# Shifting the SBUF pools of a decoder layer by pads: activations on multiples of 64 bytes, weight tiles 32 bytes off

## Chip, core and metric

The kernel is one layer of a decoder and runs on one core of a Trainium2 chip. The metric is the device time of the whole kernel in microseconds; lower is better. Everything is computed in float32; matmuls take operands of type float32r, and each product is made of three (high x high, high x low, low x high) to keep the precision, so every matrix is held as a high and a low part.

## What is computed

The reference, cut to what matters (one sequence of 1024 tokens, width 1024, 8 heads, depth 1):

```python
h = rms_norm(x, attn_norm_w)
q, k, v, u, g = jnp.split(h @ w_in, splits, axis=-1)
q, k = rms_norm(q, q_norm_w), rms_norm(k, k_norm_w)      # per head, two halves of 64
a = diff_attention(q[0], q[1], k[0], k[1], v, lam, rel_bias)   # softmax 1 - lam * softmax 2
a = rms_norm(a, subln_w) * (1.0 - lam_init)
y_a = a @ w_proj_attn
u_a, u_b = jnp.split(u, 2, axis=-1)
c = causal_depthwise_conv(u_a * sigmoid(u_b), conv_w, conv_b)   # width 31
y_b = silu(layer_norm(c, conv_ln_w, conv_ln_b)) @ w_proj_conv
g_a, g_b = jnp.split(sigmoid(g + gate_b), 2, axis=-1)
x = x + (g_a * y_a + g_b * y_b) @ w_out
gt, up = jnp.split(rms_norm(x, ffn_norm_w) @ w_gate_up, 2, axis=-1)
return x + (silu(gt) * up) @ w_down
```

## The kernel before

A matmul here multiplies a moving tile (streamed, 128, 256 or 512 columns) with a stationary tile of 128 x 128 (the weights of TensorE, loaded by a LDWEIGHTS that may run beside the matmul before it). Two helpers issue nearly all of them through `mm3` (lines 144 to 146, three matmuls: high x high, high x low, low x high of the two operands, each step of k):

- `gemm_T(w, mhi, mlo, sb)`: the matrix from DRAM (whi, wlo) is stationary, the activations move, 512 columns. It serves the U items (convolution input, 8 items, each 2 x 2 x 24 matmuls), the G items (gates, 16 items of 2 x 24), the two projections (aT and cT, 384 each), and the first three gate and up blocks of the FFN (288).
- `gemm_N(o, halves, shi, slo, i)`: the activations are stationary and whi, wlo move, 256 columns. It serves the V items (4 of 192), the Q items (8 of 192) and the output projection (mT, 768).

The FFN's other 19 blocks run in `pair` (products in line 1153), which makes four blocks of the gate and up products out of seven products of 12 matmuls each: three with parts of h2 moving (h2 is the normalised second input, tiles h_hi and h_lo), three with the differences T1 to T3 moving against weights split into whi and wlo, and one with T4 moving against weights in the tiles sh and sl. The down projection (1056 matmuls) has the hidden activations in whi and wlo as weights, and sh and sl, 512 columns of w_down, moving.

The stages in order: V and U items with the first Q item (to about 330 us); attention (330 to 840), in which the scores of head h run while Q and G items of later heads fill TensorE's gaps; the projection of the attention (840 to 940); that of the convolution (940 to 1030); the output projection (1030 to 1130); the second norm (to 1145) and the FFN (1145 to 1575); the down projection (to the end).

In attention a step (h, i) issues: `scores`, two score matmuls per 512 keys (sc, weights qs, moving ks, lines 684 and 685), a reduction on VectorE (E, mn), an exponential on ScalarE (E, l, line 691) and their difference on VectorE; `turn`, transposes of E (pT) and their split into ph (ScalarE, line 111) and pl (VectorE, line 116); every second step `weigh` (pW, moving ph and pl, weights vh and vl), and two steps later `back`, a transposition (pB) whose result ScalarE scales into an (line 748) and squares with a row sum (line 749). A Q item projects q and k of a head: after each bank pg of 512 columns ScalarE copies it to qkraw (line 563) and squares it in eight parts of 64 columns, with row sums (line 566); the bank is free again when the last of the eight is done. In attention two banks go round for pg. The squares themselves are never read, only their sums are: they go to scratch tiles, jk in `q_item` and jk2 in `back`, one buffer each, in the pool sm.

The program is recorded in the order of the code, and a scheduler then orders the instructions of each engine, within the dependencies of the tiles. Two instructions that write the same buffer of sm keep the order in which they were recorded.

Where tiles lie: SBUF pools are laid one behind the other in the order in which they are opened, from the left (cst, big, wp, sm, and then the pool of the stage: a0, attn, b1, fp), or one ahead of the other from the right end (the convolution's, then q and k; later aT and mT; later the differences T). In the program as built, hT_hi begins at byte 18368 of each partition, hT_lo at 51136 (cT and h2 take the same places later), wraw at 83904, whi at 92096, wlo at 104384, sg at 116672; the first tile of the stage's pool on the left is at 123552, and aT, mT and T begin at 163808. Divided by 64, hT, cT, h2, wraw, whi, wlo and sg leave 0; all tiles of the stage pools on the left (E, ph, vh, sh, sl and others) and all on the right (aT, mT, T, qs, ks) leave 32. Every operand of a matmul lies a multiple of 512 bytes behind the start of its tile, so the remainder of the tile is that of the operand.

Of the kernel before, what the change touches and what calls it, by code (L numbers as in the profile page):

```python
# [9 lines left out]
F32 = mybir.dt.float32  # L10
F32R = mybir.dt.float32r
AF = mybir.ActivationFunctionType
# [3 lines left out]
P = 128  # L16
# [3 lines left out]
HD = 64  # L20
VD = 128
# [33 lines left out]
def kernel(  # L55
# [36 lines left out]

    cst = ctx.enter_context(tc.tile_pool(name="cst", bufs=1))
    big = ctx.enter_context(tc.tile_pool(name="big", bufs=1, reuse_waits="tile"))
    wp = ctx.enter_context(tc.tile_pool(name="wp", bufs=3, reuse_waits="tile"))
    sm = ctx.enter_context(tc.tile_pool(name="sm", bufs=4))
    dr = ctx.enter_context(tc.tile_pool(name="dr", bufs=1, space=bass.MemoryType.DRAM))
    ps = ctx.enter_context(tc.tile_pool(name="ps", bufs=2, space=PSUM))

    bg = Spread()  # L100
    uid = [0]

    def nm(s):
        uid[0] += 1
        return f"{s}_{uid[0]}"

    def f32(ap):
        return ap.bitcast(F32)
# [21 lines left out]
    def pg():  # L130
        npg[0] += 1
        p_, tag = pgs[npg[0] % len(pgs)]
        return p_.tile([P, 512], F32, tag=tag, name=nm("pg"))
# [4 lines left out]
    def pm(z="pm"):  # L138
        npm[0] += 1
        p_, tag = pms[npm[0] % len(pms)]  # L140
        return p_.tile([P, 512], F32, tag=tag, name=nm(z))
# [53 lines left out]
    def pcol(key, k=0):  # L195
        c = col[key] + k
        return pvec[:, c : c + 1]
# [104 lines left out]
    def gemm_T(w, mhi, mlo, sb):  # L302

        o = pg()
        cs = slice(sb * 512, (sb + 1) * 512)
        for k in range(NKT):
            mm3(o[:], w[0][:, k, :], w[1][:, k, :], kt(mhi, k)[:, cs], kt(mlo, k)[:, cs], k == 0, k == NKT - 1)
        return o

    def gemm_N(o, halves, shi, slo, i):  # L310

        ts = slice(i * P, (i + 1) * P)
        for k in range(NKT):
            whi, wlo = halves[k // 4]
            mm3(o, kt(shi, k)[:, ts], kt(slo, k)[:, ts], whi[:, k % 4, :], wlo[:, k % 4, :], k == 0, k == NKT - 1)
# [153 lines left out]
    def rstd_of(ss, n, scale, fast=False):  # L469
        v = sm.tile([P, 16], F32, tag="v", name=nm("v"))[:, :n]  # L470
        dve.tensor_scalar(v, ss, scale, EPS, op0=ALU.mult, op1=ALU.add)
        return rsq(v, n, fast)
# [79 lines left out]
    def q_item(h):  # L552
        halves = [ws.next(), ws.next()]
        t = {}
        T[h] = t
        for b in range(2):
            raw = qkp.tile([P, 4, 256], F32, tag="qkraw", name=nm("qkraw"), bufs=2)
            ss = sm.tile([P, 16], F32, tag="ss16", name=nm("ss16"))
            for i2 in range(2):
                o = pg()  # L560
                for e in range(2):
                    gemm_N(o[:, 256 * e : 256 * (e + 1)], halves, hT_hi, hT_lo, 4 * b + 2 * i2 + e)
                act.copy(raw[:, 2 * i2 : 2 * i2 + 2, :], o[:].rearrange("p (e c) -> p e c", c=256))
                jk = sm.tile([P, HD], F32, tag="jk", name=nm("jk"), bufs=1)
                for g in range(8):
                    act.activation(
                        jk[:], o[:, g * HD : (g + 1) * HD], AF.Square, accum_out=ss[:, 8 * i2 + g : 8 * i2 + g + 1]
                    )
                if i2 == 0:
                    yield  # L570
            r = rstd_of(ss[:], 16, 1.0 / HD, fast=h > 0)
            r4 = raw[:].rearrange("p i (g d) -> p (i g) d", d=HD)
            dve.tensor_tensor(r4, r4, r.unsqueeze(2).to_broadcast([P, 16, HD]), op=ALU.mult)

            def turn_qk(b=b, raw=raw):


                dma = nc.sync.dma_start
                for z, key in enumerate(("q", "k")):
                    pt = pm("pQ")  # L580
                    for i in range(4):
                        pe.transpose(pt[:, i * P : (i + 1) * P], raw[:, i, z * P : (z + 1) * P], ident[:])  # L582
                    w = pcol(key + "n")

                    def part(j):
                        return qkp.tile([P, 512], F32R, tag=f"{key}s{j}", name=f"{key}s{j}_{h}_{b}", bufs=2 if key == "q" else 3)

                    s1, s2 = part(1), part(2)
                    act.activation(s1[:], pt[:], AF.Identity, scale=w)
                    lo = part(3) if key == "q" else qkp.tile([P, 512], F32R, tag="klo", name=f"klo_{h}_{b}", bufs=1)  # L590
                    dve.scalar_tensor_tensor(lo[:], pt[:], w, f32(s1[:]), op0=ALU.mult, op1=ALU.subtract)
                    dma(f32(s2[HD:, :]), f32(s1[HD:, :]))
                    if key == "q":
                        lo2 = part(4)
                        for one, two in ((s1, s2), (lo, lo2)):
                            if one is lo:
                                dma(f32(two[HD:, :]), f32(one[HD:, :]))
                            dma(f32(two[:HD, :]), f32(one[HD:, :]))
                            dma(f32(one[HD:, :]), f32(one[:HD, :]))
                        t["q", b] = (s1, lo), (s2, lo2)  # L600
                    else:
                        dma(f32(s2[:HD, :]), f32(lo[HD:, :]))
                        dma(f32(s1[HD:, :]), f32(lo[:HD, :]))
                        t["k", b] = s1, s2

            late.append((NT * h if b and h else 0, turn_qk))
            yield

    inatt = [False]
    MAKE = {"V": v_item, "U": u_item, "Q": q_item, "G": g_item}  # L610

    def run(items):
# [124 lines left out]
    def back(h, b, ar):  # L737
        pt = pm("pB")
        for e in range(2):
            pe.transpose(pt[:, e * P : (e + 1) * P], ar[:, e * P : (e + 1) * P], ident[:])  # L740
        if h not in AN:
            AN[h] = aps.tile([P, NT, VD], F32, tag="an", name=f"an{h}", bufs=1)
            SSA[h] = sm.tile([P, NT], F32, tag="ssa", name=nm("ssa"))
        jk = sm.tile([P, VD], F32, tag="jk2", name=nm("jk2"), bufs=1)
        for e in range(2):
            i = 2 * b + e
            src, r = pt[:, e * P : (e + 1) * P], RL[h][:, i : i + 1]
            act.activation(AN[h][:, i, :], src, AF.Identity, scale=r)
            act.activation(jk[:], src, AF.Square, scale=r, accum_out=SSA[h][:, i : i + 1])
# [42 lines left out]
    def slot(n, nq):  # L792

        with after(last_fill[0]):
            for h, b, ar in ready(backs, n):
                back(h, b, ar)
                if b == NT // 2 - 1:
                    subln(h)
                    sublns.append((n + 1, h))
            for _ in range(nq):  # L800
                if late[0][0] <= n:
                    late.pop(0)[1]()
            for h in ready(sublns, n):
                subln_T(h)
            for h, b in ready(weighs, n):
                backs.append((n + 2, (h, b, weigh(h, b))))
                if b == NT // 2 - 1 and h + 1 < H:
                    load_v(h + 1)
# [153 lines left out]
    def gated(d, cs):  # L962
        g = bp.tile([P, 512], F32, tag="gt", name=nm("gt"), bufs=4)
        nc.sync.dma_start(g[:], d[:, cs])
        act.activation(g[:], g[:], AF.Sigmoid)
        return g
# [29 lines left out]
    for cl in ((0, 1, 2), (3, 4), (5, 6), (7,)):  # L996
        pair = [(c, ws.next()) for c in cl]
        for sb in range(2):
            cs = slice(sb * 512, (sb + 1) * 512)
            for c, w in pair:  # L1000
                g = gated(g_d[NKT + c], cs)
                ya = bp.tile([P, 512], F32, tag="ya", name=nm("ya"), bufs=4)
                nc.sync.dma_start(ya[:], ya_d[c][:, cs])
                o = gemm_T(w, cT_hi, cT_lo, sb)
# [32 lines left out]
    for z, (j, half) in enumerate(WO):  # L1037
# [3 lines left out]
        for i2 in (2 * half, 2 * half + 1):  # L1041
            o = pg()
# [22 lines left out]
    def acc():  # L1065
        nacc[0] += 1
        p_, tag = banks[nacc[0] % 4]
        return p_.tile([P, 512], F32, tag=tag, name=nm("acc"))
# [172 lines left out]
    for n in range(2):  # L1241
        o = [acc() for i in range(NT)]
# [62 lines left out]
```

## Time and profile before

| what | value |
|---|---|
| median of 3 runs | 1830.63 us (1829.6 to 1832.09) |
| profiled execution | 1831.76 us, span 1830.0 us |
| TensorE matmul busy | 1800.7 us (98%), 9895 records |
| TensorE weight load busy | 1556.9 us (85%) |
| VectorE, ScalarE, GpSimd busy | 1237.2, 752.8, 26.6 us |
| granted TensorE clock, mean | 0.993 |
| DMA queue of SyncE | 40.4% of 16 engines' span |

The span is the time from the first to the last profiled instruction of one execution; 1.8 us of its time lie outside. Matmuls are pipelined: each record lasts some 280 ns (256 columns) or 390 ns (512), but the next one begins before it ends. What a matmul costs in a dense stretch is therefore the distance from its start to the next start, which a window of a pure stage gives as its length divided by the number of matmuls in it. The mean duration of a group moves with the distance, since the part that overlaps stays nearly the same. "Idle before" is the time in which the engine had nothing to do ahead of a group's instructions, with what ended it.

### The profile page before, as it was taken

To read this page: it belongs to the slowest core of one execution; us is meant where nothing else is said; L and a number is where in the kernel's file an instruction comes from. 1 tells how busy PE (TensorE), PEld (TensorE's weight loads), DVE (VectorE), ACT (ScalarE), POOL (GpSimd) and SP (SyncE) were. 2 spreads that over 40 slices of the span, in tenths; PEclk is the share of its full clock that TensorE was granted. 3 is DMA by queue.
4 is the path that set the end of the run, shared out by engine and by line. 5 is a ranking of instruction groups with operands and counts; after the bars stand their busy time and mean duration, and the time that the engine had idled before them with its cause. 6 is when DMAs were issued, how large, how long until landed. Compare 5 with 4: busy or idle time off the path is not lost.

```text
span 1830.0 us, 26409 instructions
## 1 busy us (share of the span) xinstructions
PE 1800.7 (98%) x9895; PEld 1556.9 (85%) x9895; DVE 1237.2 (68%) x2157; ACT 752.8 (41%) x1814; POOL 26.6 (1%) x106
## 2 busy tenths in 40 slices
PE   7999999999999999999999999999999999899998
PEld 6899998999898989987888998788888888788887
DVE  6388789999888998884885337965565655433433
ACT  5211331667676876664473114322222222222221
POOL 3000000000000000000000000000000000000000
PEclk9999999999999999999999999999999999999999
DMA  8433273233544354436945424122232232544643
GB/s 243 153 116 121 93 208 103 81 103 110 139 127 126 93 135 125 119 106 236 304 135 157 157 93 139 58 84 77 75 96 72 75 98 69 184 138 138 230 140 113
DMA packets 218032, 236.56 MB, mean 129 GB/s; under 512 B 12160, under 2 KB 157608, under 8 KB 217904
## 3 DMA queue, kind: packets, MB, share of 16 engines
q1 hardware_dynamic: 215872, 228.64, 40.4%
q0 software_dynamic: 1744, 5.19, 1.0%
q8 instruction: 78, 1.28, 0.3%
q10 hardware_dynamic: 288, 1.05, 0.2%
q14 instruction: 50, 0.41, 0.1%
HBM read 158.24 MB, written 58.23 MB: 118 GB/s over the span
## 4 chain that ended last, share of the span: by engine, by line
PE 95%; DMA 2%; DVE 1%; ACT 1%; issue 0%; SPq 0%; ACTq 0%; DVEq 0%
PE acc L1153 20%; PE pg L144 17%; PE pg L146 17%; PE pg L145 17%; PE acc L144 5%; PE acc L145 4%; PE acc L146 4%; PE sc L685 2%; PE sc L684 2%; PE pT L720 2%; PE pW L144 1%; PE pW L146 1%; PE pW L145 1%; PE pQ L582 1%; DMA wraw<-in_w_in_dram 1%; PE pS L761 0%
## 5 line engine op out<-in xcount | busy, mean ns | idle before, releaser
L111 ACT CAST whi<-wraw 128x1024 fp32r<-128x1024 f32 x153 | 160.6, 1050 | 432.4 <-PE acc L145 159.3
L116 DVE TENSOR_TENSOR wlo<-wraw,whi 128x1024 fp32r<-128x1024 f32 x153 | 187.0, 1222 | 194.3 <-ACT whi L111 194.2
L393 DVE SCALAR_TENSOR_TENSOR acc<-u,cw,acc 128x1024 f32<-128x1024 f32 x240 | 306.9, 1279 | 2.8
L144 PE MATMUL pg<-whi,hT_hi 128*128 128x256 f32 x768 | 221.1, 288 | 0.1
L146 PE MATMUL pg<-whi,hT_lo 128*128 128x256 f32 x768 | 221.0, 288 | 0.1
L145 PE MATMUL pg<-wlo,hT_hi 128*128 128x256 f32 x768 | 220.2, 287 | 0.0
L144 PE MATMUL pg<-hT_hi,whi 128*128 128x512 f32 x512 | 201.3, 393 | 0.0
L145 PE MATMUL pg<-hT_lo,whi 128*128 128x512 f32 x512 | 201.1, 393 | 0.0
L146 PE MATMUL pg<-hT_hi,wlo 128*128 128x512 f32 x512 | 200.6, 392 | 0.0
L144 PEld LDWEIGHTS pg<-whi,hT_hi 128*128 128x128 f32 x768 | 148.2, 193 | 3.1 <-ACT gr L541 0.6
L146 PEld LDWEIGHTS pg<-whi,hT_lo 128*128 128x128 f32 x768 | 148.2, 193 | 2.7 <-DVE hT_lo L116 0.7
L145 PEld LDWEIGHTS pg<-wlo,hT_hi 128*128 128x128 f32 x768 | 148.2, 193 | 1.7 <-DVE wlo L116 0.3
L144 PE MATMUL acc<-sh,whi 128*128 128x512 f32 x352 | 138.7, 402 | 4.0 <-ACT sh L111 4.0
L145 PE MATMUL acc<-sl,whi 128*128 128x512 f32 x352 | 139.8, 397 | 0.0
L146 PE MATMUL acc<-sh,wlo 128*128 128x512 f32 x352 | 139.6, 397 | 0.0
L691 ACT ACTIVATE E<-E,mn 128x256 f32<-128x256 f32 (+7 forms) x128 | 99.9, 782 | 37.3 <-DVE mn L686 36.6
L146 PEld LDWEIGHTS pg<-hT_hi,wlo 128*128 128x128 f32 x512 | 96.2, 188 | 19.2
L144 PEld LDWEIGHTS pg<-hT_hi,whi 128*128 128x128 f32 x512 | 96.3, 188 | 18.9
L145 PEld LDWEIGHTS pg<-hT_lo,whi 128*128 128x128 f32 x512 | 96.3, 188 | 18.6
L111 ACT CAST whi<-s 128x1024 fp32r<-128x1024 f32 x38 | 39.9, 1049 | 142.3 <-PE acc L1153 108.3
L1153 PE MATMUL acc<-h_lo,whi 128*128 128x512 f32 x228 | 89.4, 392 | 0.0
L1153 PE MATMUL acc<-h_hi,whi 128*128 128x512 f32 x228 | 89.3, 392 | 0.0
(258 smaller groups left out, 4023.8 us busy)
## 6 DMA issues: line engine op xcount, KB each, us to landing
wraw<-in_w_gate_up_dram SPq DMA_DIRECT2D x44, 512.0 KB, 4.6
wraw<-gu_d SPq DMA_DIRECT2D x44, 512.0 KB, 3.7
wraw<-in_w_in_dram SPq DMA_DIRECT2D x40, 512.0 KB, 4.1
qs<-qs SPq DMA_DIRECT2D x96, 128.0 KB, 2.3
rd<-in_w_down_dram SPq DMA_DIRECT2D x44, 256.0 KB, 3.7
wraw<-in_w_in_dram SPq DMA_DIRECT2D x32, 256.0 KB, 3.5
g_d<-sgg SPq DMA_DIRECT2D x32, 256.0 KB, 2.2
gt<-g_d SPq DMA_DIRECT2D x32, 256.0 KB, 3.7
```

The source lines that it names most:

```text
L111: act.copy(dst, src)
L116: last_lo[0] = dve.tensor_tensor(dst, src, f32(hi), op=ALU.subtract).ins
L144: pe.matmul(o, lh, rh, start=start, stop=False)
L145: pe.matmul(o, lh, rl, start=False, stop=False)
L146: last_mm[0] = pe.matmul(o, ll, rh, start=False, stop=stop).ins
L393: dve.scalar_tensor_tensor(acc[0][:], us[c][:, t : t + S], cw[:, c, t : t + 1], acc[0][:], op0=ALU.mult, op1=ALU.add)
L582: pe.transpose(pt[:, i * P : (i + 1) * P], raw[:, i, z * P : (z + 1) * P], ident[:])
L684: pe.matmul(o[:, :w], qh[:, qs], k, start=True, stop=False)
L685: last_mm[0] = pe.matmul(o[:, :w], ql[:, qs], k, start=False, stop=True).ins
L691: act.activation(e[:, :nk], e[:, :nk], AF.Exp, bias=mn[:, j : j + 1], scale=-1.0, accum_out=l[:, j : j + 1])
L720: pe.transpose(pt[:, k * P : (k + 1) * P], e[:, (k0 + k) * P : (k0 + k + 1) * P], ident[:])
L1153: pe.matmul(o[:], a_[x_][:, k, :], b_[y_][:, k, :], start=start and k + x_ + y_ == 0, stop=k == 3 and x_ == 1, skip_group_check=not start,)
```

## The change

Three pads are added, and the two scratch tiles become one.

- A pool `shift` between big and wp holds one tile of 8 floats (32 bytes): wp and all behind it move by 32.
- cst gets 16 floats (64 bytes) more, at its start: big and all behind it move by 64.
- A pool `edge` of 24 floats (96 bytes) is the first on the right: all tiles on the right move down by 96.
- jk in `q_item` is now 128 columns wide, of which the first 64 are used, and jk in `back` has the same tag, so both share one buffer of 512 bytes where 256 and 512 bytes stood: what lies behind sm moves by -256.

```diff
     big = ctx.enter_context(tc.tile_pool(name="big", bufs=1, reuse_waits="tile"))
+    shift = ctx.enter_context(tc.tile_pool(name="shift", bufs=1))
+    shift.tile([P, 8], F32, name="pad_weights")
     wp = ctx.enter_context(tc.tile_pool(name="wp", bufs=3, reuse_waits="tile"))
...
+    cst.tile([P, 16], F32, name="pad_left")
+    edge = ctx.enter_context(tc.tile_pool(name="edge", bufs=1, side="right"))
+    edge.tile([P, 24], F32, name="pad_right")
...
-                jk = sm.tile([P, HD], F32, tag="jk", name=nm("jk"), bufs=1)
+                jk = sm.tile([P, VD], F32, tag="jk", name=nm("jk"), bufs=1)[:, :HD]
                 for g in range(8):
                     act.activation(
-                        jk[:], o[:, g * HD : (g + 1) * HD], AF.Square, accum_out=ss[:, 8 * i2 + g : 8 * i2 + g + 1]
+                        jk, o[:, g * HD : (g + 1) * HD], AF.Square, accum_out=ss[:, 8 * i2 + g : 8 * i2 + g + 1]
                     )
...
-        jk = sm.tile([P, VD], F32, tag="jk2", name=nm("jk2"), bufs=1)
+        jk = sm.tile([P, VD], F32, tag="jk", name=nm("jk"), bufs=1)
```

In the program as built, hT_hi then begins at 18432 and hT_lo at 51200, wraw at 84000, whi at 92192, wlo at 104480, sg at 116768, the stage's pool on the left at 123392, and aT, mT and T at 163712. Divided by 64, hT, cT and h2 leave 0 as before; wraw, whi, wlo and sg leave 32; the stage pools on the left and all tiles on the right leave 0. No instruction is added or removed. On TensorE, VectorE, ScalarE and SyncE the order differs from the one before in the attention stage, on TensorE first at the beginning of head 1, and in some places behind it up to the first products of the FFN; ahead of head 1 and behind those products nothing is moved but addresses. Lines behind the pads have numbers higher by 7.

## Prediction

> **What bounds the kernel now.** I read the page's busy shares and its chain first, then the stages by windows, then the matmul groups, then single matmuls.
>
> ```profile
> PE 1800.7 (98%) x9895; PEld 1556.9 (85%) x9895; DVE 1237.2 (68%) x2157; ACT 752.8 (41%) x1814; POOL 26.6 (1%) x106
> PE 95%; DMA 2%; DVE 1%; ACT 1%; issue 0%; SPq 0%; ACTq 0%; DVEq 0%
> ```
>
> TensorE is busy 98% of the span and carries 95% of the chain that ends last. All other engines together leave it idle for 1830.0 - 1800.7 = 29.3 us. So the time is the sum of the distances from one matmul to the next, and the change is worth what it does to those. Stages that are pure in one kind of matmul give the distance (the window, its length, PE busy with the count, then the other engines):
>
> ```profile
> 255.00:315.00 60.00, 60.00 (x266) 49.71 (x265) 51.79 (x46) 10.13 (x13) 0.60 (x4) 1.00 0.45 136
> 330.00:840.00 510.00, 506.64 (x3380) 463.92 (x3380) 444.33 (x1029) 343.92 (x1173) 11.69 (x65) 1.00 0.41 113
> 945.00:1025.00 80.00, 80.00 (x354) 66.28 (x353) 47.99 (x68) 35.06 (x53) 0.00 (x0) 1.00 0.44 138
> 1150.00:1195.00 45.00, 45.00 (x198) 37.19 (x197) 40.95 (x39) 13.98 (x17) 0.00 (x0) 0.99 0.19 59
> 1225.00:1560.00 335.00, 335.00 (x1453) 272.55 (x1452) 192.82 (x256) 92.47 (x120) 0.00 (x0) 1.00 0.27 82
> 1600.00:1820.00 220.00, 220.00 (x945) 177.35 (x944) 74.08 (x84) 59.80 (x76) 0.00 (x0) 1.00 0.44 150
> 162.00:183.00 21.00, 21.00 (x177) 21.00 (x176) 19.17 (x18) 2.04 (x5) 0.00 (x0) 1.00 0.35 113
> 1032.00:1098.00 66.00, 66.00 (x560) 66.00 (x559) 20.80 (x50) 9.80 (x12) 0.00 (x0) 1.00 0.41 144
> ```
>
> A record counts if any part of it lies in the window. A 512-column record lasts some 390 ns, so I take 1.7 off the count (390 / 227), and 2.4 for 256 columns (288 / 120). Then 512 columns take 60,000 / 264.3 = 227.0 ns with hT moving (255 to 315 us), 227.1 with cT, 229.2 with h2 in the gates, 230.8 in the FFN products, and 220,000 / 943.3 = 233.2 with sh and sl moving in the down projection. 256 columns take 120.3 ns with hT as weights and 118.4 with mT as weights. The clock is full in all of them and no window has PE idle but the attention's (3.4 us).
>
> Same shapes, different distances: what differs is where the two operands lie. I call a matmul **equal** if its moving tile and the weights loaded while it runs (those of the next matmul) start at the same remainder by 64 bytes, and **opposite** if the remainders differ by 32. In the kernel before, hT, cT, h2, whi and wlo are at 0; aT, mT, T, sh, sl, ph, vh, qs, ks and E at 32. The groups (busy us, mean ns of one):
>
> ```profile
> L145 PE MATMUL pg<-hT_lo,whi 128*128 128x512 f32 x512 | 201.1, 393 | 0.0
> L145 PE MATMUL pg<-cT_lo,whi 128*128 128x512 f32 x128 | 49.9, 390 | 0.0
> L145 PE MATMUL pg<-aTl,whi 128*128 128x512 f32 x128 | 50.8, 397 | 0.0
> L145 PE MATMUL acc<-sl,whi 128*128 128x512 f32 x352 | 139.8, 397 | 0.0
> L1153 PE MATMUL acc<-h_lo,whi 128*128 128x512 f32 x228 | 89.4, 392 | 0.0
> L1153 PE MATMUL acc<-T1l,whi 128*128 128x512 f32 x76 | 30.1, 396 | 0.0
> L145 PE MATMUL pg<-wlo,hT_hi 128*128 128x256 f32 x768 | 220.2, 287 | 0.0
> L145 PE MATMUL pg<-wlo,mTh 128*128 128x256 f32 x256 | 72.3, 282 | 0.0
> L145 PE MATMUL pW<-pl,vh 128*128 128x256 f32 x160 | 46.4, 290 | 0.0
> ```
>
> (Behind <- the moving tile comes first, the weights second.) With 512 columns, equal rows have 390 to 393 ns and opposite rows 396 to 397. With 256 it turns round: opposite (mT) 282, equal (hT, pW) 287 to 290.
>
> All these 512-column opposite rows have the moving tile at 32 and the weights at 0; the change makes the mirror image. The mirror image exists before only at seams. These are single matmuls, each asked for in a window of its own: two of cT, the last of cT, whose next weights are mT (32), and two of hT, the second followed by a score with weights qs (32).
>
> ```profile
> L144 PE MATMUL pg<-cT_hi,whi 128*128 128x512 f32 x1 | 0.4, 389 | 0.0
> L145 PE MATMUL pg<-cT_lo,whi 128*128 128x512 f32 x1 | 0.4, 389 | 0.0
> L146 PE MATMUL pg<-cT_hi,wlo 128*128 128x512 f32 x1 | 0.4, 397 | 0.0
> L146 PE MATMUL pg<-hT_hi,wlo 128*128 128x512 f32 x1 | 0.4, 389 | 0.0
> L145 PE MATMUL pg<-hT_lo,whi 128*128 128x512 f32 x1 | 0.4, 397 | 0.0
> ```
>
> The moving tile is the same; only the next weights have moved by 32, and the matmul is 8 ns longer. So I read the cost as one of opposite remainders, whichever side is shifted.
>
> **The change part by part.** The pads are allocated and never used: no instruction, no cost. They do what they say: hT, cT, h2 stay at 0 (18432 = 288 x 64), whi and wlo go to 32 (92192 = 1440 x 64 + 32), all pools behind them and on the right go to 0. So nearly every matmul becomes opposite.
>
> (a) 512 columns, equal to opposite, to 233.2 ns. U items, 768 matmuls x (233.2 - 227.0) = +4.8 us. Gate items, 768, in the attention stage, among scores and transposes: no window isolates them. Their group with U has 393 ns against 390 in pure stages, so the G half has some 396, against 397 for opposite rows: a lower bound of 1 ns, an upper one of 6.2; I take 4, +3.1, because the group's mean also holds matmuls that wait after transposes. cT, 384 x 6.1 = +2.3. Gates of the FFN, 288 x (233.2 - 229.2) = +1.2. Products: 19 pairs x 84 = 1596; of seven products three move h (equal now), three T against whi (opposite now), one T4 against sh. Afterwards six are opposite and T4 equal: (6 x 233.2 + 227) / 7 = 232.3 against 230.8, +2.4. Sum +13.8 (from 9 to 18, with every row at its lower or upper end).
>
> (b) 256 columns with hT as weights, equal to opposite: 118.4 - 120.3 = -1.9 ns. 960 outside attention, -1.8; 1344 inside, where I take half, -1.3. Sum -3.1 (from -4.4 to 0).
>
> (c) Opposite before, mirrored after: aT 384, sh 1056, mT 768: 0, give or take 2 ns each, 4 us. pW, scores and transposes: under 1 us.
>
> (d) ScalarE, VectorE and the queues also read shifted tiles. Before, both remainders exist:
>
> ```profile
> L111 ACT CAST whi<-wraw 128x1024 fp32r<-128x1024 f32 x153 | 160.6, 1050 | 432.4 <-PE acc L145 159.3
> L111 ACT CAST whi<-s 128x1024 fp32r<-128x1024 f32 x38 | 39.9, 1049 | 142.3 <-PE acc L1153 108.3
> rd<-in_w_down_dram SPq DMA_DIRECT2D x44, 256.0 KB, 3.7
> gt<-g_d SPq DMA_DIRECT2D x32, 256.0 KB, 3.7
> ```
>
> wraw and rd lie at 0, s and gt at 32, and the times agree: 0.
>
> (e) The scratch tile. The squares of q_item and of back write two tiles before and share one after. Nobody reads it, but its users must now run in the order of the program, and the scheduler moves the attention stage to fit. ScalarE near the end of head 0, before (qkraw is the copy of a projected bank pg, jk are its squares, E the exponentials of head 0):
>
> ```order
> L563 COPY qkraw_3835<-pg_3837 128x512
> L566 ACTIVATE jk_3887,ss_418_3836<-pg_3837 128x64 x3
> L691 ACTIVATE E_3623,l_3622<-E_3623,mn_3621 128x1024
> L566 ACTIVATE jk_3887,ss_418_3836<-pg_3837 128x64 x5
> L691 ACTIVATE E_3633,l_3622<-E_3633,mn_3621 128x1024
> ```
>
> The same place in the changed kernel, where that bank is called pg_3846 and its copy stands 17 rows ahead of its squares (an and jk from pB are back's scaling and squares, qs a part of the queries):
>
> ```order
> L755 ACTIVATE an_3430<-pB_3743,rl_0_2951 128x128
> L756 ACTIVATE jk_3746,ssa_3431<-pB_3743,rl_0_2951 128x128
> L755 ACTIVATE an_3430<-pB_3743,rl_0_2951 128x128
> L698 ACTIVATE E_3820,l_3813<-E_3820,mn_3812 128x256
> L756 ACTIVATE jk_3746,ssa_3431<-pB_3743,rl_0_2951 128x128
> L573 ACTIVATE jk_3896,ss_418_3845<-pg_3846 128x64
> L596 ACTIVATE qs_1_1_3756<-pQ_3751,pvec 128x512
> ```
>
> The eight squares that free the bank now stand behind back's. TensorE at the same place, before (pg the projection of the next Q item, sc the scores of head 1):
>
> ```order
> L146 MATMUL pg_3926<-whi_3547,hT_lo 128x256
> L144 MATMUL pg_4052<-whi_3379,hT_hi 128x256
> L145 MATMUL pg_4052<-wlo_3380,hT_hi 128x256
> L146 MATMUL pg_4052<-whi_3379,hT_lo 128x256
> L684 MATMUL sc_3812<-ks_1_0_3230,qs_1_0_3213 128x256
> L685 MATMUL sc_3812<-ks_1_0_3230,qs_1_0_3218 128x256
> ```
>
> TensorE there in the changed kernel (pT are transposes of E):
>
> ```order
> L153 MATMUL pg_3935<-whi_3556,hT_lo 128x256
> L691 MATMUL sc_3821<-ks_1_0_3239,qs_1_0_3222 128x256
> L692 MATMUL sc_3821<-ks_1_0_3239,qs_1_0_3227 128x256
> L727 MATMUL pT_3729<-ident,E_3632 128x128 x4
> L691 MATMUL sc_3919<-ks_1_0_3238,qs_1_0_3221 128x384
> ```
>
> The next bank's projection comes only 42 rows further on. Until then TensorE has ten score matmuls, transposes and the 24 of pW, some 7 us by the distances above. ScalarE has in that stretch, by the groups of the attention stage, a copy qkraw, three ph, four E (each with a read of the accumulator, 0.2 us), two each of an and of back's squares, qs, ks and ar, 7 to 9 us, and eight squares at 0.35 us (the starts of two), 2.8 us:
>
> ```profile
> L563 ACT COPY qkraw<-pg 128x512 f32<-128x512 f32 x27 | 15.8, 586 | 13.1 <-PE pg L146 13.1
> L111 ACT CAST ph<-pT 128x512 fp32r<-128x512 f32 x48 | 28.1, 586 | 27.3 <-PE pT L720 26.6
> L691 ACT ACTIVATE E<-E,mn 128x384 f32<-128x384 f32 x16 | 9.9, 618 | 0.8 <-DVE mn L686 0.7
> L749 ACT ACTIVATE jk<-pB,rl 128x128 f32<-128x128 f32 x64 | 24.3, 379 | 0.0
> L589 ACT ACTIVATE qs<-pQ,pvec 128x512 fp32r<-128x512 f32 x14 | 9.6, 686 | 3.4 <-PE pQ L582 3.4
> ```
>
> ```profile
> 384.45 0.23 ACT L566 ACTIVATE jk<-pg 128x64 f32<-128x64 f32 x1
> 384.80 0.23 ACT L566 ACTIVATE jk<-pg 128x64 f32<-128x64 f32 x1
> ```
>
> That is 10 to 12 us against 7, partly begun earlier, so I estimate that TensorE waits some 3 us there. One other stretch without projection is as long in the new order (5.7 us of work, in head 5, also ten scores); others are as before. I take +5 us for both (0 if TensorE's slower matmuls give ScalarE the time, 12 if every Q item pays 2).
>
> Sum: 13.8 - 3.1 + 5 = +15.7. The profiled execution took 1831.76 us (span 1830.0), 1.1 above the median of the runs, 1830.63. 1831.76 + 15.7 = 1847.5 for it, 1846.3 for the median. A difference under 0.2% (3.7 us) counts as none.
>
> **The rivals.** *One side only (faster).* The cost lies in a moving tile at 32, and the seams above are a first matmul out of step, not a steady state. Then all 512-column matmuls go to 227.0: down projection and aT 1440 x -6.2 = -8.9, products 1596 x (227.0 - 230.8) = -6.1, nothing gained on 256 columns; with the order's +5, 1820.6; if the 256-column gain of mT holds for all, near 1811. For it: mT's weights at 32 under a moving tile at 0 are the fastest 256-column row. Against it: the seams at 397. It decides from a steady distance of about 230.3 ns down, where (a), (b) and (e) cancel. Chance 0.16.
>
> *No effect of place.* The groups differ by stage, not by address, and only (e) is left: 1830.6 to 1835.6. Against it: the seam of cT, where no stage changes. Chance 0.08. The Trainium skill, "SBUF — State Buffer", section "Who interferes with whom", gives this result: it lists separate read ports for the moving operand and the weights, and says that PE never waits on anyone. By that rule nothing happens; the rows of 390 and 397 do not agree with it.
>
> *The scratch tile at every head.* Seven Q items x 3 us = 21 instead of 5: 1862. For it: the rows above repeat with each Q item; against it: only two long stretches appear. Chance 0.08.
>
> **How the numbers follow.** Forecast 0.68, with a range of its own from 1836 (9 from (a), -4.4 from (b), 1 from (e)) to 1857 (18, 0 and 9). Predicted is its 1846.3. Down to 1826 the range takes in the second rival and the edge of the first, up to 1860 the lower part of the third. Faster 0.16 (first rival), same 0.09 (most of the second, the forecast's low end), slower 0.75.
>
> **What would show it.** The window with hT moving should show 233 ns instead of 227, cT's rows 396 to 397, hT's 256-column rows about 282, the down projection unchanged at 397; the attention window more PE idle than 3.4 us. I am wrong if cT's rows stay at 390 or fall, or if sl's rows fall to 390.

## The result and the profile after

| what | before | after |
|---|---|---|
| median of 6 runs each | 1830.61 us (1829.27 to 1832.09) | 1840.22 us (1837.35 to 1842.14) |
| profiled execution, its span | 1831.76, 1830.0 us | 1838.79, 1837.0 us |

The change makes the kernel slower: ratio 1.0051 with a 95% interval of [1.0038, 1.0064], +9.6 us by the medians. The two profiled executions lie only 7.0 us apart: the one of before is 1.2 us above its median, the one of after 1.4 below; their mean granted clocks are 0.993 and 0.995.

The page after, first the span, then the busy shares, then the chain that ends last:

```profile
span 1837.0 us, 26407 instructions
PE 1808.2 (98%) x9895; PEld 1547.7 (84%) x9895; DVE 1237.8 (67%) x2157; ACT 753.5 (41%) x1814; POOL 26.7 (1%) x106
PE 96%; DMA 2%; ACT 1%; DVE 1%; issue 0%; SPq 0%; ACTq 0%; DVEq 0%
```

TensorE's busy time grew by 7.5 us, the span by 7.0, and the rest (1837.0 - 1808.2 = 28.8 us) is what it was (29.3). So TensorE did not wait more; its matmuls, as many as before, took longer. The stages by windows, in the order hT, V (256 columns), attention, cT, mT, products, down projection:

```profile
255.00:315.00 60.00, 60.00 (x259) 48.32 (x258) 51.08 (x45) 9.28 (x12) 0.47 (x3) 1.00 0.44 138
164.00:184.00 20.00, 20.00 (x174) 20.00 (x173) 18.49 (x18) 1.77 (x3) 0.00 (x0) 1.00 0.35 119
330.00:840.00 510.00, 506.84 (x3390) 460.37 (x3389) 444.76 (x1032) 345.51 (x1182) 11.72 (x65) 1.00 0.40 113
950.00:1030.00 80.00, 80.00 (x344) 64.41 (x344) 46.25 (x67) 31.99 (x49) 0.00 (x0) 1.00 0.40 129
1036.00:1100.00 64.00, 63.62 (x542) 63.42 (x542) 18.59 (x48) 8.51 (x10) 0.00 (x0) 1.00 0.42 147
1230.00:1565.00 335.00, 335.00 (x1438) 269.92 (x1437) 191.61 (x254) 92.03 (x119) 0.00 (x0) 1.00 0.26 82
1605.00:1825.00 220.00, 220.00 (x945) 177.10 (x943) 75.02 (x86) 59.71 (x76) 0.00 (x0) 1.00 0.43 152
```

Counted as in the prediction, 512 columns now take 60,000 / 257.3 = 233.2 ns with hT (227.0 before), 233.7 with cT (227.1), 335,000 / 1436.3 = 233.2 in the products (230.8), and 233.2 in the down projection, as before. 256 columns take 20,000 / 171.6 = 116.6 ns with hT as weights (120.3) and, by the busy time, 63,620 / 539.6 = 117.9 with mT (118.4). The groups of after say the same in their mean durations:

```profile
L152 PE MATMUL pg<-hT_lo,whi 128*128 128x512 f32 x512 | 203.0, 397 | 0.0
L152 PE MATMUL pg<-cT_lo,whi 128*128 128x512 f32 x128 | 50.6, 395 | 0.0
L152 PE MATMUL acc<-sl,whi 128*128 128x512 f32 x352 | 139.9, 397 | 0.0
L1160 PE MATMUL acc<-h_lo,whi 128*128 128x512 f32 x228 | 90.0, 395 | 0.0
L1160 PE MATMUL acc<-T4l,sh 128*128 128x512 f32 x76 | 30.0, 395 | 0.0
L152 PE MATMUL pg<-wlo,hT_hi 128*128 128x256 f32 x768 | 217.0, 283 | 0.0
L152 PE MATMUL pg<-wlo,mTh 128*128 128x256 f32 x256 | 72.0, 281 | 0.0
```

All rows that had 390 to 393 ns now have 395 to 397; the 256-column row of hT fell from 287 to 283; sl and mT stand where they stood. The stages, each from its first matmul to that of the next, show where the 7.0 us came from (the last column is what the prediction's terms make for that stage):

| stage | before | after | difference | forecast |
|---|---|---|---|---|
| V, U, first Q item | 319.1 | 321.7 | +2.6 | +4.8 - 1.8 |
| attention | 529.9 | 527.6 | -2.3 | +3.1 - 1.3 + 5 |
| projection of the attention (aT) | 94.2 | 94.2 | 0 | 0 |
| of the convolution (cT) | 87.1 | 89.6 | +2.5 | +2.3 |
| output projection (mT) | 94.4 | 94.6 | +0.2 | 0 |
| second norm and FFN gates | 80.8 | 81.4 | +0.6 | +1.2 |
| FFN products | 370.9 | 374.5 | +3.6 | +2.4 |
| down projection | 253.6 | 253.4 | -0.2 | 0 |

Outside attention the forecast says +8.9 and the two executions +9.3. Attention was to become 6.8 us longer and became 2.3 shorter. Some 1.7 us of the 2.3 lie in the clock: the profile of before has a stretch of 3.4 us there in which the granted clock was 0.51 (the column behind 0.00 (x0)), the profile of after has none:

```profile
820.00:823.40 3.40, 3.33 (x15) 3.33 (x16) 0.62 (x2) 1.06 (x6) 0.00 (x0) 0.51 0.00 0
```

TensorE's waits in the attention window (engine, what waited, line, for whom: us in total, times, longest), after:

```profile
PE sc L691 <- DMA ks<-klo: 1.3, 1, 1.3
PE sc L691 <- DVE mn L693: 0.8, 1, 0.8
PE pB L747 <- DVE pl L123: 0.5, 1, 0.5
PE pW L151 <- ACT jk L756: 0.3, 1, 0.3
PE pT L727 <- DVE pl L123: 0.2, 1, 0.2
```

3.2 us of idle time in all, against 3.4 before; the wait for the scratch (jk) is 0.3 us.

### The profile page after: what moved, and what is told of

It is laid out like the page before. It is cut to its first block, busy times and chain, and to the rows that moved or that the text cites. A ratio compares the mean times of both kernels' runs of the same rounds, so it can differ in the third digit from the quotient of the medians.

```text
span 1837.0 us, 26407 instructions
## 1 busy us (share of the span) xinstructions
PE 1808.2 (98%) x9895; PEld 1547.7 (84%) x9895; DVE 1237.8 (67%) x2157; ACT 753.5 (41%) x1814; POOL 26.7 (1%) x106
## 4 chain that ended last, share of the span: by engine, by line
PE 96%; DMA 2%; ACT 1%; DVE 1%; issue 0%; SPq 0%; ACTq 0%; DVEq 0%
PE acc L1160 20%; PE pg L151 17%; PE pg L153 17%; PE pg L152 17%; PE acc L151 4%; PE acc L152 4%; PE acc L153 4%; PE sc L692 2%; PE sc L691 2%; PE pT L727 1%; PE pW L153 1%; PE pW L152 1%; PE pW L151 1%; DMA xt<-in_x_dram 1%; PE pQ L589 1%; PE pB L747 0%
## 5 line engine op out<-in xcount | busy, mean ns | idle before, releaser
L1160 PE MATMUL acc<-h_hi,wlo 128*128 128x512 f32 x228 | 90.0, 395 | 0.0
```

The costliest lines, as they stand in the source:

```text
L1160: pe.matmul(o[:], a_[x_][:, k, :], b_[y_][:, k, :], start=start and k + x_ + y_ == 0, stop=k == 3 and x_ == 1, skip_group_check=not start,)
```

## The experiments

Three readings stood at the start. *Place alone*: the whole cost comes from where the moving tile and the next weights lie to each other, and the order is worth nothing. *The prediction's split*: place and order both cost, in the proportion 10.7 to 5. *Order as a gain*: attention became shorter in after, so the order helps and the place costs more than the total. Then, when the place was shown, the question became which pairs of places are good. Times are medians beside runs of the kernel before on the same chip; nothing that is computed changes in any of these kernels, the scratch being read by nobody.

### The order alone

**scratch_only** merges the two scratch tiles as the change does and puts back the bytes that this saves. Its order of instructions is that of after, its addresses those of before.

```diff
+    sm.tile([P, HD], F32, tag="hold", name="hold", bufs=1)
...
-                jk = sm.tile([P, HD], F32, tag="jk", name=nm("jk"), bufs=1)
+                jk = sm.tile([P, VD], F32, tag="jk", name=nm("jk"), bufs=1)[:, :HD]
...
-        jk = sm.tile([P, VD], F32, tag="jk2", name=nm("jk2"), bufs=1)
+        jk = sm.tile([P, VD], F32, tag="jk", name=nm("jk"), bufs=1)
```

> Only the shared scratch tile, all addresses as before, so the order of the changed kernel over the remainders of before. The prediction's term (e): +5 us, 1835.6, with TensorE waiting some 3 us twice in the attention stage. Theory now (the order is worth nothing, only the remainders count): 1830.6, within 2 us. Rival (the order gains what the attention stage of the changed kernel shows, 2.2 us, or more): 1826 to 1828.

1832.96 us (11 runs) against 1831.01 (17 runs): ratio 1.0012 [1.0003, 1.0021], so +2.2 us, between 0.5 and 3.8. The attention window:

```profile
330.00:840.00 510.00, 505.66 (x3374) 460.63 (x3373) 444.28 (x1031) 343.89 (x1180) 11.66 (x65) 1.00 0.42 112
```

TensorE is idle for 4.3 us of it, 0.9 more than before. The order costs something, so it is neither a gain nor worth nothing, but less than half of the 5 us put down for it, and it is the smaller part of the 9.6.

### The addresses alone

**pads_only** keeps the two scratch tiles, and with them the order of before, and reaches the change's remainders by 64 with two pads.

```diff
+    shift = ctx.enter_context(tc.tile_pool(name="shift", bufs=1))
+    shift.tile([P, 8], F32, name="pad_shift")
...
+    edge = ctx.enter_context(tc.tile_pool(name="edge", bufs=1, side="right"))
+    edge.tile([P, 8], F32, name="pad_right")
```

> Only the remainders of the changed kernel (weights' tiles at 32, all others at 0), two scratch tiles and the order of before. Theory now: all of the slowdown is here, 1840 (1838 to 1842). The prediction's split (addresses +10.7, order +5), scaled to what was measured: 1837. If the order were what gains: above 1842.

1837.96 us (5 runs), ratio 1.0035 [1.0022, 1.0048]: +6.4 us, between 4.0 and 8.8, nearest to the split. Windows with hT moving, and of the products; and two of its groups:

```profile
255.00:315.00 60.00, 60.00 (x259) 48.36 (x258) 50.97 (x45) 8.63 (x11) 0.47 (x3) 1.00 0.45 136
...
1230.00:1565.00 335.00, 335.00 (x1443) 270.99 (x1442) 191.10 (x253) 91.25 (x119) 0.00 (x0) 1.00 0.27 81
```

```profile
L1157 PE MATMUL acc<-T1l,whi 128*128 128x512 f32 x76 | 30.1, 396 | 0.0
L1157 PE MATMUL acc<-T4l,sh 128*128 128x512 f32 x76 | 29.6, 390 | 0.0
```

With not one instruction moved, hT is at 60,000 / 257.3 = 233.2 ns: the cause is the address. The two parts make 0.12% + 0.35% = 0.47%, and the change as a whole 0.51%: within the intervals nothing is left over. One row differs: T4 against sh has 390 ns here and 395 in after, though in both the two tiles leave the same remainder by 64. By 256 bytes they start 0 apart here and 128 apart in after. So pads_only is the change's addresses by 64, but not by 256; the output projection (weights and mT 224 apart by 256 here, 96 in after) is shorter too, 93.2 us instead of 94.6.

The page of before already had a row against the rule of the prediction. T4 and sh are equal by 64 there as well (both at 32), lie 192 apart by 256, and this row was among the slow ones:

```profile
L1153 PE MATMUL acc<-T4l,sh 128*128 128x512 f32 x76 | 30.0, 395 | 0.0
```

### All at one remainder: 0, and 32

**all_at_0** undoes the offset altogether: one pad behind the pools on the left that come first, one on the right, both of 8 floats; the order is that of before. Every operand of TensorE then lies at remainder 0 by 64, and all but the identity matrix of the transposes at the same remainder by 256 too. **all_at_32** puts every one at remainder 32 by 64, with scratch tiles of half the size to make room.

```diff
+    tail = ctx.enter_context(tc.tile_pool(name="tail", bufs=1))
+    tail.tile([P, 8], F32, name="pad_tail")
+    edge = ctx.enter_context(tc.tile_pool(name="edge", bufs=1, side="right"))
+    edge.tile([P, 8], F32, name="pad_right")
```

```diff
+    cst.tile([P, 8], F32, name="pad_left")
...
+    tail = ctx.enter_context(tc.tile_pool(name="tail", bufs=1))
+    tail.tile([P, 8], F32, name="pad_tail")
...
+                jk = sm.tile([P, HD], mybir.dt.bfloat16, tag="jk", name=nm("jk"), bufs=1)
...
+        jk = sm.tile([P, VD], mybir.dt.bfloat16, tag="jk2", name=nm("jk2"), bufs=1)
```

> Order of before, every tile that TensorE reads at a multiple of 64, the weights' tiles too. Theory (equal remainders are fast for 512 columns, whichever they are): aT and the down projection 1440 x (226.8 - 233.2) = -9.2, products 1596 x (226.8 - 230.8) = -6.4, mT 768 x (120.0 - 118.4) = +1.2, sum -14.4: 1816. Rival (the distance depends on the stage and on what moves, not on the pair of addresses): 1830.6.

> Order of before, every tile that TensorE reads 32 bytes behind a multiple of 64 (room is made by writing the scratch of the squares, which nobody reads, in bf16). Theory (only the difference of the two remainders counts): as with all at 0, 1816. Rival (a tile off a multiple of 64 costs by itself, moving or stationary): all 512-column matmuls at 233 ns, some 2900 x 6.4 = +18 us, 1849.

all_at_0: 1815.57 us (4 runs), ratio 0.9914 [0.9901, 0.9928], where 1816 was expected; it is faster than both kernels. all_at_32: 1825.62 us (6 runs), 0.9972 [0.9961, 0.9983], where 1816 was expected as well. The groups of all_at_0:

```profile
L149 PE MATMUL acc<-sl,whi 128*128 128x512 f32 x352 | 137.1, 390 | 0.0
L149 PE MATMUL pg<-aTl,whi 128*128 128x512 f32 x128 | 50.1, 392 | 0.0
L1157 PE MATMUL acc<-T4l,sh 128*128 128x512 f32 x76 | 29.6, 390 | 0.0
```

And of all_at_32:

```profile
L148 PE MATMUL acc<-sl,whi 128*128 128x512 f32 x352 | 139.8, 397 | 0.0
L148 PE MATMUL pg<-aTl,whi 128*128 128x512 f32 x128 | 50.1, 392 | 0.0
L1156 PE MATMUL acc<-T4l,sh 128*128 128x512 f32 x76 | 30.1, 396 | 0.0
```

In all_at_32 aT improved as expected, but sl stayed at 397. There sh and sl start 128 bytes from the weights by 256, aT does not. So "equal by 64" fell as a rule, twice (here and with T4 above); what fits both is "equal by 256".

### Which differences are good

Two kernels, each executed once, move the weights inside wider tiles. **sweep** takes another offset with every sixth pair of splits, **constant_steps** one offset for a whole item, so that hundreds of successive matmuls have one difference (the start of the weights loaded next less that of the moving tile, by 256 bytes). constant_steps also has one buffer for the tile at of attention, to make room, which in the program as built changes the order of TensorE's instructions from attention on.

```diff
+    nw = [0]
...
+        off = nw[0] // 6 % 4 * 4
+        nw[0] += 1
+        hi = wp.tile([P, 1040], F32R, tag="whi", name=nm("whi"))[:, off : off + 1024]
+        lo = wp.tile([P, 1040], F32R, tag="wlo", name=nm("wlo"))[:, off : off + 1024]
```

```diff
+    def wsplit(raw, off=0):
+        hi = wp.tile([P, 1088], F32R, tag="whi", name=nm("whi"))[:, off : off + 1024]
+        lo = wp.tile([P, 1088], F32R, tag="wlo", name=nm("wlo"))[:, off : off + 1024]
...
+            return ld_wide(win, [(V0 + 256 * c, 256)], (4, 16, 32, 48)[c])
...
+            o = (4, 12, 16, 24, 32, 40, 48, 60)[c]
+            return ld_cols(win, U0 + D + c * P, o) + ld_cols(win, U0 + c * P, o)
...
+        ws.plan(ld_cols(wpc, c * P, (0, 0, 0, 2, 2, 1, 1, 20)[c]))
...
+            ws.plan(ld_wide(wout, [(256 * j, 256)], (8, 4, 24, 56)[j]))
```

> Order of before; the weights' tiles whi and wlo are 64 bytes longer, and each split uses them from byte 0, 16, 32 or 48, six splits each in turn, so that the start of the weights minus the start of the moving tile takes all multiples of 16 up to 512 bytes (scratch in bf16 for room). Theory 1 (remainders by 64): 512 columns at 226.7 ns for differences of 0, 64, 128, 192 and at 233 for 32, 96, 160; that contradicts all_at_32, where sh and sl, 128 bytes apart from the weights, took 233 ns at equal remainders by 64. Theory 2 (what counts is the difference by 256): 226.7 at 0 and 256, 229 at 64 and 192, 233 at 32, 128, 160 and 224; what 16 does, neither tells. The whole kernel then takes 1832 to 1840, since few matmuls are left at 0.

> Order of work as before; each item keeps one difference between weights and moving tile, by 256, through all its matmuls: the U items 16, 48, 64, 96, 128, 160, 192 and 240 bytes, cT 0, 8, 4 and 80, the V items (256 columns) 16, 64, 128, 192, the output projection 0, 16, 192 and 64 (for room the scratch is bf16 and the tile at has one buffer instead of two). Theory 2 (difference by 256): U at 64 and 192 near 229 ns, at 128 and 160 near 233. Theory 1 (by 64): U at 64, 128 and 192 at 226.7. Theory 3, from the sweep's mean of 231 to 232 at every difference: a constant difference makes its own steady distance; the seams at 397 ns are then only the step out of it, and values other than 226.7 and 233.3 appear. For 4, 8 and 16 bytes none of them gives a number. The total says nothing here.

sweep took 1835.81 us beside 1828.62 for before and told nothing about single differences: with the difference changing every few matmuls, each of them came to 229 to 233 ns on average, 0 among them (232). Even rows that had been at 397 move to the middle, and hT's row rises from 393:

```profile
L145 PE MATMUL pg<-hT_lo,whi 128*128 128x512 f32 x512 | 202.3, 395 | 0.0
L145 PE MATMUL acc<-sl,whi 128*128 128x512 f32 x352 | 138.9, 395 | 0.0
```

So the good distance showed only where the difference stays. constant_steps, 1845.64 us beside 1828.0, gives the distances of successive starts, in the steady part of each item:

| difference by 256 | 512 columns, ns | 256 columns, ns |
|---|---|---|
| 0 | 226.8 | 120.0 |
| 4, 8 | 232.4, 230.7 | |
| 16 | 233.3 | 117.1 |
| 32 (from the trace of after; before) | 233.3 | 118.3 |
| 48, 64 | 233.3, 233.3 | at 64: 117.8 and 113.3 |
| 80, 96 | 232.0, 234.3 | at 96 (after): 117.3 |
| 128 | 233.4 | 120.0 |
| 160, 192 | 233.4, 228.9 | at 192: 117.8 |
| 224, 240 | 233.4, 228.4 | at 224 (after): 116.7 |

Windows of it, with differences of 128 and 192 under hT, 0 under cT, then 256 columns with 0, 16 and 64:

```profile
189.00:209.00 20.00, 20.00 (x88) 16.08 (x87) 16.52 (x16) 2.88 (x4) 0.12 (x1) 1.00 0.50 152
281.00:301.00 20.00, 20.00 (x89) 16.44 (x88) 19.68 (x18) 2.37 (x4) 0.00 (x0) 1.00 0.25 78
956.00:987.00 31.00, 31.00 (x138) 25.46 (x137) 24.88 (x38) 21.42 (x34) 0.00 (x0) 1.00 0.30 95
1045.00:1066.00 21.00, 21.00 (x177) 21.00 (x176) 5.48 (x10) 0.85 (x3) 0.00 (x0) 1.00 0.66 251
1068.00:1089.00 21.00, 21.00 (x181) 21.00 (x181) 4.24 (x10) 0.96 (x2) 0.00 (x0) 1.00 0.16 51
1101.50:1111.00 9.50, 9.50 (x86) 9.50 (x85) 5.71 (x25) 3.17 (x6) 0.00 (x0) 1.00 0.66 221
```

In 20 us one record more or less makes 2.6 ns, so here the windows only bear the table out roughly: 31,000 / 136.3 = 227.4 at 0, 20,000 / 86.3 = 231.7 at 128, 9,500 / 83.6 = 113.6 for the fastest 256 columns. Of the differences tried, none was as good as 0 for 512 columns; for 256 columns 0 and 128 were the worst.

### Weights of the 256-column stages moved for themselves

If 512 columns want 0 and 256 columns anything else, a kernel can have both: all at one remainder, and whi and wlo moved by some bytes where they are the moving tile of 256 columns (V, Q, output projection). **wide_0** is the control (tiles of 1088 floats, one buffer for at, scratch of half the size, nothing moved), **wide_32** moves them by 32 bytes, **wide_64** puts all else at 224 by 256 and the moved weights at 160. The edit of wide_32, cut (wsplit as in constant_steps):

```diff
+    tail.tile([P, 40], F32, name="pad_tail")
...
-    def ld_wide(w, cols):
+    def ld_wide(w, cols, off=8):
...
-                hi, lo = wsplit(raw)
+                hi, lo = wsplit(raw, off)
...
-            at = aps.tile([P, 512], F32, tag="at", name=nm("at"), bufs=2)
+            at = aps.tile([P, 512], F32, tag="at", name=nm("at"), bufs=1)
```

> Control for the next two: every tile that TensorE reads starts at the same remainder by 256 (192), two scratch tiles in bf16, the tile at with one buffer, weights' tiles 256 bytes longer. Theory (the difference by 256 alone sets the distance): as all at 0, 1815.6, if the one buffer costs nothing.

> As the control, but where whi and wlo move (256 columns, V, Q and output projection), they are used from byte 32 on; 512-column matmuls keep difference 0. Theory: 256 columns go from 120.0 to 116.8 ns, 3072 x -3.2 = -9.8 us against the control: 1806. Rival (256-column stages are bound by the weight loads or by something else that does not move with addresses): as the control.

> As wide_32, but the moving weights lie 64 bytes ahead of the stationary tile by 256 (moving at 160, stationary at 224), as in the fourth part of the output projection of constant_steps, which took 113.3 ns, and not as in its fourth V item, 117.8 ns at the same difference from other starts (128 and 192). Theory A (the difference and the starts by 64 count): 113.3 ns everywhere, 3072 x -6.7 = -20.5 us against the control: 1795. Theory B (113.3 was a steady state of that one stage): 117.8, -6.8 us: 1809.

| kernel | us (runs) | ratio to before |
|---|---|---|
| wide_0 | 1822.43 (5) | 0.9955 [0.9943, 0.9968] |
| wide_32 | 1818.45 (5) | 0.9928 [0.9914, 0.9941] |
| wide_64 | 1815.68 (4) | 0.9912 [0.9897, 0.9927] |

The control missed 1815.6 by 7 us. The attention window, first of all_at_0, then of wide_0:

```profile
330.00:840.00 510.00, 507.31 (x3381) 464.87 (x3380) 443.85 (x1028) 344.52 (x1174) 11.72 (x65) 1.00 0.41 114
```

```profile
330.00:840.00 510.00, 502.25 (x3357) 459.89 (x3356) 443.07 (x1028) 342.27 (x1175) 11.61 (x65) 1.00 0.41 112
```

TensorE is idle for 7.7 us instead of 2.7, and the stage took 536.1 us against 529.0. What differs there is at's second buffer, with the order that follows from it, and the tiles' width; the first is the likely cause, but it was not tried alone. wide_32 should have gained 9.8 us on the control and gained 4.0. Its output projection, and that of wide_64, as windows:

```profile
1029.00:1094.00 65.00, 65.00 (x560) 65.00 (x558) 20.69 (x50) 9.73 (x12) 0.00 (x0) 1.00 0.41 146
```

```profile
1032.00:1099.00 67.00, 67.00 (x572) 67.00 (x571) 22.05 (x53) 10.64 (x13) 0.00 (x0) 1.00 0.40 142
232.00:248.00 16.00, 16.00 (x143) 16.00 (x143) 15.23 (x21) 4.52 (x19) 0.00 (x0) 1.00 0.76 204
```

wide_32 has its 116.6 ns (65,000 / 557.6), as expected. wide_64 has 67,000 / 569.6 = 117.6 in the output projection and 16,000 / 140.6 = 113.8 in the first Q item: two steady distances at one and the same difference of 64 by 256, the two that constant_steps shows as well. Its total, 6.7 us under the control, is near what 117.8 ns everywhere would give (6.8). What decides between them was not found out. Most of the 6 us that wide_32's median lacks lie in the granted clock. Its five runs had 0.992 to 0.995 on average, the control's 0.994 to 0.997. A run's span times its granted clock, an estimate of the span at a full clock, gives 1802 to 1804 us for wide_32 and 1810 to 1813 for wide_0; the means are 8.3 us apart, of 9.8 expected. The profiled execution of wide_32 (1813.19 us) is the fastest of its five (up to 1820.56), 11 us under the control's, and has every moved stage at its expected distance. One row of it looks as if the rule failed: aT, 0 apart from its weights, has 395 ns in wide_32 against 391 in wide_0. The window says otherwise:

```profile
845.00:867.00 22.00, 21.10 (x83) 16.68 (x84) 16.84 (x25) 13.55 (x22) 0.00 (x0) 0.92 1.04 376
```

The granted clock was 0.92 in this window, at the beginning of that stage, and 1.00 in the same stage of wide_0: a mean over a group mixes the place of the tiles with such a dip, so rows are compared where the clock is full. wide_64 settles one point for good. It has the down projection's operands at remainder 32 by 64, as all_at_32 has, but 0 apart by 256:

```profile
L148 PE MATMUL acc<-sl,whi 128*128 128x512 f32 x352 | 137.7, 391 | 0.0
L1156 PE MATMUL acc<-T4l,sh 128*128 128x512 f32 x76 | 29.6, 389 | 0.0
```

391 instead of 397: it is the difference by 256 that counts here, not the remainder itself.

## Why the prediction was right, and where it was not

The direction and the mechanism held: the addresses alone make the kernel slower (pads_only), through the distance of matmuls and not through waits. The sum was 15.7 and the measured change 9.6, inside the forecast's range of 1836 to 1857 us. Term by term:

- **Reading the bound.** Right. Idle time of TensorE stayed within 0.5 us, and the change came out in its busy time.
- **The mirror image costs the same (a).** Right for U and cT: 233.2 and 233.7 ns where 233.2 was forecast. U is 768 x 6.2 = +4.8 as forecast, cT's stage +2.5 for +2.3. The seams at 397 were indeed the steady state to come. The rival of one side only fell with cT's 395, and that no place matters fell with pads_only; the rule that this rival takes from the Trainium skill ("SBUF — State Buffer", section "Who interferes with whom") does not account for these 6.2 ns.
- **The gates of the FFN in (a).** The price was misread. Not in all windows was the clock full: that of the gates has 0.99, since its first 1.1 us lie at the end of a stretch at half the granted clock, and so 229.2 ns came out. Windows of before and after behind these stretches give 45,000 / 198.3 = 226.9 and 36,000 / 154.3 = 233.3 ns, so 288 x 6.4 = +1.8 instead of +1.2. The stage itself shows only +0.6, with a half-clock stretch of 10.2 us in the profile of before (1140.9 to 1151.1) and of 6.8 in that of after (1145.6 to 1152.4). The two windows:

```profile
1152.00:1197.00 45.00, 45.00 (x200) 37.26 (x199) 40.92 (x39) 13.85 (x16) 0.00 (x0) 1.00 0.19 59
1153.00:1189.00 36.00, 36.00 (x156) 29.02 (x155) 32.40 (x30) 11.45 (x14) 0.00 (x0) 1.00 0.21 67
```

- **The rule "equal by 64" behind (a).** Wrong, though it hardly touched the sum. 512 columns are good at 0 by 256. Of before's equal rows those with hT, cT and h2 lay so; T4 against sh did not (192 apart), had 395 ns in the row shown above, and I left it out of the comparison. After the change, "equal" again, it was taken at 227 ns; it lies 128 apart and still has 395 ns in that row. So all seven products are slow: 233.2 instead of 232.3 ns, +3.6 for the stage instead of +2.4.
- **The 256 columns (b).** Mis-sized. I took mT's 118.4 as the goal of hT; it reached 116.6. I took the difference by 64 for the whole of it; by 256, mT lay 32 from its moving tile and hT now lies 224 from it, the difference at which wide_32 shows 116.6 too. With 120.3 - 116.6 = 3.7 ns, the 960 outside attention give -3.6 instead of -1.8.
- **G and Q in attention.** No window isolates them, but the traces have the start of every matmul. Between successive matmuls of Q in attention (pairs up to 140 ns apart) the mean distance is 119.1 ns before and 117.0 after, between those of G (up to 260 ns) 229.2 and 232.8. So Q is mis-sized and G is not: as estimates, 1344 x -2.1 = -2.8 instead of -1.3, and 768 x 3.6 = +2.8 instead of +3.1. The two cancel, so by these terms the addresses leave attention as long as it was.
- **The stage of V and U.** That it came out at +2.6 where +3.0 was forecast is luck. With (b) as measured its terms make 4.8 - 3.6 = +1.2; the profile of after has 1.7 us more of TensorE waiting in its first 20 us (for the first hT_hi, and with no releaser that the profile shows). scratch_only, with the addresses of before, has such waits too, 1.0 and 1.6 us, so the addresses of the change are not needed for them.
- **The same before and after (c, d).** Right: aT's stage 94.2 and 94.2, mT's +0.2, the down projection -0.2. Busy times of VectorE and ScalarE moved by less than 1 us.
- **The scratch tile (e).** The order was read rightly and its price was not: +2.2 us (0.5 to 3.8) instead of +5. I set 10 to 12 us of ScalarE's work against 7 of TensorE's and let 3 remain at the next projection. In the profile of after TensorE's stretch, from its first score (395.56 us) to the next projection (404.96), lasts 9.4 us, with two waits in it. ScalarE is busy from 395.04 us on, and the sum of the eighth square, which frees the bank, is read just before that projection:

```profile
398.52 0.50 PE L691 MATMUL sc<-ks,qs 128*128 128x512 f32 x1 [0.77 <-DVE mn L693]
400.10 0.38 PE L151 MATMUL pW<-ph,vh 128*128 128x256 f32 x1 [0.26 <-ACT jk L756]
404.67 0.24 ACT L573 ACTIVATION_READ_ACCUMULATOR jk<-pg 128x1 f32 x1
404.96 0.39 PE L151 MATMUL pg<-whi,hT_hi 128*128 128x256 f32 x1
```

That is 1.0 us of waiting, and none on record when the projection comes. What failed is the step from the two lists to 3 us: TensorE's stretch has 8.4 us without its waits, not 7, and ScalarE was through after 9.9, not 10 to 12. scratch_only shows the same two waits, 0.8 and 0.2 us; where the rest of its 2.2 us lies is not shown. The sign named for (e), more idle time in the attention window than 3.4 us, appeared in scratch_only (4.3) and not in after (3.2). The rival that put 3 us at every head fell with the 2.2.

The first rival's second figure, near 1811, comes out of its terms only without the order's +5; with it they make 1816.

With the measured terms the sum is, as an estimate, 4.8 + 2.5 + 1.8 + 3.6 - 3.6 outside attention (9.1), 0 for G and Q, +2.2 for the order: 11.3, inside the measured 7.0 to 11.7 us (the interval of the ratio). The 4.4 us that the forecast has above that are (b), 3.3, and (e), 2.8, less 1.7 that (a) fell short. For pads_only the 9.1 us of the addresses, less 1.4 for T4 (228 x 6.2 ns) and 1.2 for mT (93.2 us instead of before's 94.4), make 6.5, and 6.4 were measured.

Open: why a difference of 0 by 256 holds successive matmuls of 512 columns at 226.8 ns; why 256 columns know two distances at one difference. What the rest of all_at_0 would gain from moved 256-column weights with both buffers of at was not tried: there was no room in SBUF.

## What to carry to other kernels

Where TensorE is busy without a gap, look at the distance of starts by stage; if stages of one shape differ by some 3%, compare where the moving tile and the next weights start. Of what was tried here, all operands at one remainder by 256 bytes was best for 512 columns (all_at_0: -0.86%, for two pads of 32 bytes), while 256 columns preferred a difference; so a pairing has to be tried at both shapes. A dependency that only moves work on an engine with slack costs at most what that engine's list exceeds the other's by, so both lists have to be added up with care: here 1.4 us missing from TensorE's list and too much in ScalarE's made 3 us of waiting out of 1.

## What the runs showed of the hardware

- One matmul of 512 columns in fp32r takes 226.8 ns from start to start when the moving tile and the next weights start 0 apart by 256 bytes, and mostly 231 to 234 otherwise, at a full clock; 4 bytes of difference are enough (232.4). 192 and 240 lie between (228.9, 228.4).
- The 226.8 ns showed only with a difference that stays: with alternating ones, 512 columns averaged 229 to 233 ns, those of 0 included (sweep).
- 256 columns behave the other way: 120.0 ns at 0 and 128, 116.7 to 118.3 at the others, and at a difference of 64 now 117.8 and now 113.3.
